# Stick-breaking's projections: the fourth pair's upper parts of q and k bound behind the rounding of the next column's weights

## The chip, the core and the metric

The kernel runs on one core of a Trainium2 chip. Its engines work side by side, each through its own list of instructions in order: TensorE (PE in the profile) multiplies matrices into PSUM, VectorE (DVE), ScalarE (ACT) and GpSimd (POOL) work elementwise, SyncE (SP) issues transfers; GpSimd's list holds transfers too. An instruction starts when its engine has come to it and the semaphores that it waits for have reached their values. The metric is the device time in microseconds, as the median of several runs.

## The reference

One layer of a hybrid decoder, 1024 real tokens and 16 meta tokens of width 1024, all in float32:

```python
h = h + 0.5 * swiglu(rms_norm(h, ffn1_norm), ffn1_w_in, ffn1_w_out)
u = rms_norm(h, mix_norm) @ w_in
hq, hf, hi, hg, sq, sk, sv = split(u)            # seven groups of 512 columns
o_hg = hgrn2(hq, hf, hi, hg, ...)                # 4 heads of 128, gated recurrence
o_sb = stick_breaking(sq, sk, sv, q_gain, k_gain)  # 8 heads of 64
h = h + concat(o_hg, o_sb) @ w_out
h = h + 0.5 * swiglu(rms_norm(h, ffn2_norm), ffn2_w_in, ffn2_w_out)
```

Stick-breaking normalizes q and k by head (`q = rms_norm(q, q_gain)`), forms scores `z = q k / 8`, and weights each earlier key with sigmoid(z) times the product of sigmoid(−z) over the keys between.

## The kernel before

Every float32 product is made of three products of rounded parts: an operand is split into an upper part (rounded, written by ScalarE) and a lower part (the rest, written by VectorE). For weights this is `split_w` (L231 rounds, L233 takes the rest); the tiles are `raw` (as loaded by SP, L226, two buffers), `wh` and `wl`. `self.rounded` always holds the last rounding of weights that the program has written down.

The stage that matters here is the projection `u`, column block by column block of 128. First come stick-breaking's columns, in four pairs of heads: for each pair k, v and q (`sb_project`), each in chunks of tokens. Then come hgrn2's, head by head in the order v, f, q, g (`hgrn_fill`): a v or f column in four pieces of 264, 264, 256 and 256 tokens, a q or g column in two of 512. Two PSUM banks take turns (`proj`), so the third piece of a column needs the first piece's bank to be emptied: ScalarE copies v out (L1108), and applies sigmoids to f (L1114, L1115). The next column's weights are rounded one column ahead. The first hgrn2 column's copies are bound behind the rounding that `kept["round"]` names.

Beside the projections runs, for each pair, `sb_qk`: it transposes q and k into a layout by rows, squares and sums, takes the root on ScalarE (L1434), scales by the inverse on GpSimd (L1438), transposes back on VectorE (L1444) into the tiles `qT` and `kT`, and calls `put_split` four times (two halves of q, two of k). `put_split` writes the upper part on ScalarE (L1375, tile `ohi`, three buffers), the lower part on VectorE (L1376, `olo`), and stores both from GpSimd's list (L1379, L1380) to DRAM, from where the heads load them later. `sb_v` does the same for v through `vhl` (L1396) and stores from SP (L1404).

When two hgrn2 columns (v and f of head 0) are written down, the memory of these stages is closed and the attention proper begins (`braid`): jobs of two query blocks each, whose scores `z` (L1598), the two sigmoids (`keep` L1604, `sig` L1605), scan on VectorE (L1608) and product on GpSimd (L1614) are woven into the remaining hgrn2 columns. Its tiles take over the memory just left, with waits for whoever used it last; GpSimd first sets the last column of `keep` to one (L1593). `sig` is then turned by TensorE (`flip`, L1453) and copied out of PSUM (`wu`, L1576 and L1577).

What sets the order: on TensorE the order of the code. On the other engines a scheduler sets it when the program is built, bound by data and by edges that the code gives: `with tc.issue_after(ins)` puts the instructions of its block that run on `ins`'s engine behind `ins` in that engine's list. It is no semaphore; it moves places in a list.

Of the kernel before, what the change touches and what calls it, by code (L numbers as in the profile page):

```python
# [40 lines left out]
class Block:  # L41
# [1368 lines left out]
    def sb_qk(self, p, qT, kT, pool, mix, dst):  # L1410

        nc = self.nc
        ss, other = (
            pool.tile([P, 65], F32, tag=x, name=x, bufs=2) for x in ("sbs", "sbo")
        )
        nat = pool.tile([P, 65, 32], F32, tag="nat", name="nat", bufs=2)  # L1420
        rows = [(qT, 0, 0, 16), (qT, 512, 16, 16), (kT, 0, 32, 16), (kT, 512, 48, 17)]
        for src, c0, b0, nb in rows:
            y = nat[:, b0 : b0 + nb]
            nc.vector.transpose(y.rearrange("p b d -> p (b d)"), src[:, c0 : c0 + 32 * nb])
            sq = pool.tile([P, 17, 32], F32, tag="sq4", name="sq4", bufs=2)[:, :nb]
            nc.scalar.activation(sq, y, AF.Square)
            nc.vector.tensor_reduce(ss[:, b0 : b0 + nb], sq, mybir.AxisListType.X, ALU.add)
            yield 0, 1500
        for b in range(4):
            nc.scalar.copy(  # L1430
                other[32 * b : 32 * b + 32], ss[32 * (b ^ 1) : 32 * (b ^ 1) + 32]
            )
        nc.vector.tensor_add(ss, ss, other)
        nc.scalar.activation(ss, ss, AF.Sqrt, bias=self.eps, scale=1.0 / 64)  # L1434
        nc.vector.reciprocal(ss, ss)
        for _, _, b0, nb in rows:
            y = nat[:, b0 : b0 + nb]
            nc.gpsimd.tensor_mul(  # L1438
                y, y, ss[:, b0 : b0 + nb].unsqueeze(2).broadcast_to([P, nb, 32])
            )  # L1440
        yield 0, 6000
        for src, c0, b0, nb in rows:
            t = src[:, c0 : c0 + 32 * nb]
            nc.vector.transpose(t, nat[:, b0 : b0 + nb].rearrange("p b d -> p (b d)"))  # L1444
            n = min(32 * nb, (SEQ if src is qT else T) - c0)
            gain, to = (self.qg8, dst[0]) if src is qT else (self.kg, dst[1])
            self.put_split(to, p, slice(c0, c0 + n), t[:, :n], mix, gain)
            yield 0, 1500

    def flip(self, src, spans):  # L1450
# [887 lines left out]
```

## Time and profile before

| what | value |
|---|---|
| median of 3 runs | 1991.07 us (1990.67 to 1992.21) |
| the profiled execution's own time | 1989.35 us |
| its span, first to last instruction | 1987.6 us |
| granted TensorE clock, mean over the span | 0.997 |
| TensorE busy | 1937.9 us, 97% |
| VectorE, ScalarE, GpSimd busy | 1390.7, 854.6, 448.0 us |

A row in the order of time gives start and duration in microseconds, the engine, the line, the operation, the tiles written and read, and in brackets how long the engine stood idle before and what released it. "SPq" and "POOL DMA" rows are the issue of a transfer; the time to landing is given in the view of transfers. The projections of the fourth pair and of the first hgrn2 columns lie between about 820 and 875 us, the attention follows.

### The profile page before, as it was taken

The numbers are of one execution on the slowest core, as the hardware profiler recorded it, in microseconds if no ns is written. First come the engines' busy times: TensorE is split into PE (matmuls) and PEld (weight loads), VectorE is DVE, ScalarE is ACT, GpSimd is POOL, SyncE is SP. The second block draws the span as 40 slices with busy tenths as digits, with TensorE's granted clock in tenths as the row PEclk, the third lists the DMA queues.
The fourth block names the chain that finished last, engine by engine and source line by source line (L and its number), as shares of the span: only waits on it lengthen the run. The fifth ranks groups of instructions, "written<-read, shape, count | busy, mean of one in ns | idle before, by whom it ended". The sixth has DMA issues, their size and how long they took to land.

```text
span 1987.6 us, 30439 instructions
## 1 busy us (share of the span) xinstructions
PE 1937.9 (97%) x10768; PEld 1631.7 (82%) x10768; DVE 1390.7 (70%) x2176; ACT 854.6 (43%) x1719; POOL 448.0 (23%) x616
## 2 busy tenths in 40 slices
PE   7999999999999999989999999999999999999998
PEld 6888888888888888878898978787888888888887
DVE  7977777877677765457777667567566766767774
ACT  6523443334444444356666635433233332344443
POOL 3010100010000003133333332220544544520000
PEclk9999999999999999989999999999999999999999
DMA  7356887758965225665453176665533323278463
GB/s 210 91 168 167 254 273 241 242 183 318 374 206 187 88 73 151 153 175 146 131 152 114 58 261 188 149 228 180 185 96 106 106 96 112 101 265 302 123 195 138
DMA packets 346168, 347.16 MB, mean 175 GB/s; under 512 B 94800, under 2 KB 250320, under 8 KB 346016
## 3 DMA queue, kind: packets, MB, share of 16 engines
q1 hardware_dynamic: 325168, 283.73, 46.4%
q0 software_dynamic: 19808, 61.49, 9.0%
q8 instruction: 85, 1.39, 0.3%
q14 instruction: 67, 0.55, 0.1%
q10 hardware_dynamic: 1040, 0.00, 0.0%
HBM read 233.75 MB, written 111.38 MB: 174 GB/s over the span
## 4 chain that ended last, share of the span: by engine, by line
PE 89%; DVE 5%; ACT 2%; DMA 2%; issue 1%; POOL 1%; SPq 0%; DVEq 0%; ACTq 0%; POOLq 0%
PE o L723 21%; PE qb L448 17%; PE qa L448 12%; PE qc L448 12%; PE proj L248 5%; PE proj L250 4%; PE proj L249 4%; PE flip L1453 2%; PE wo L248 1%; PE wo L249 1%; PE wo L250 1%; PE oacc L1528 1%; PE mq L992 1%; PE oacc L1530 1%; PE lvl L1225 1%
## 5 line engine op out<-in xcount | busy, mean ns | idle before, releaser
L448 PE MATMUL qb<-T,wh 128*128 128x512 f32 x1056 | 344.4, 390 | 1.4 <-ACT T L308 0.8
L448 PEld LDWEIGHTS qb<-T,wh 128*128 128x128 f32 x1056 | 198.1, 188 | 46.1 <-issue 2.5
L448 PE MATMUL qa<-B,wh 128*128 128x512 f32 x696 | 226.7, 390 | 0.1
L248 PE MATMUL proj<-xh,wh 128*128 128x512 f32 (+2 forms) x640 | 214.2, 335 | 10.8 <-ACT st L1108 9.7
L723 PE MATMUL o<-t,w 128*128 128x512 f32 x924 | 211.8, 390 | 0.5 <-DVE u L541 0.5
L250 PE MATMUL proj<-xl,wh 128*128 128x512 f32 (+2 forms) x640 | 210.4, 329 | 0.8 <-DVE xl L1917 0.8
L249 PE MATMUL proj<-xh,wl 128*128 128x512 f32 (+2 forms) x640 | 210.4, 329 | 0.0
L723 PE MATMUL o<-parts 128*128 128x512 f32 x924 | 209.9, 389 | 0.0
L448 PE MATMUL qb<-T,wl 128*128 128x512 f32 x528 | 205.4, 389 | 0.0
L723 PEld LDWEIGHTS o<-t,w 128*128 128x128 f32 x924 | 172.8, 188 | 37.3 <-issue 0.8
L723 PEld LDWEIGHTS o<-parts 128*128 128x128 f32 x924 | 173.3, 188 | 36.0
L361 DVE TENSOR_TENSOR wl<-s,wh 128x512 fp32r<-128x512 f32 x160 | 165.7, 1035 | 50.6 <-ACT wh L359 49.7
L359 ACT CAST wh<-s 128x512 fp32r<-128x512 f32 x160 | 99.4, 622 | 193.5 <-PE qb L448 145.1
L448 PEld LDWEIGHTS qa<-B,wh 128*128 128x128 f32 x696 | 130.5, 188 | 27.6 <-DVE B L827 0.5
L248 PEld LDWEIGHTS proj<-xh,wh 128*128 128x128 f32 x640 | 121.3, 190 | 22.9 <-ACT st L1108 9.9
L359 ACT CAST wh<-raw 128x512 fp32r<-128x512 f32 x120 | 74.4, 621 | 148.3 <-PE qc L448 108.0
L448 PE MATMUL qa<-B,wl 128*128 128x512 f32 x348 | 135.5, 389 | 0.0
L250 PEld LDWEIGHTS proj<-xl,wh 128*128 128x128 f32 x640 | 121.1, 189 | 12.2 <-DVE xl L1917 1.2
L249 PEld LDWEIGHTS proj<-xh,wl 128*128 128x128 f32 x640 | 121.2, 189 | 9.9
L448 PE MATMUL qc<-T,wh 128*128 128x512 f32 x352 | 117.1, 394 | 0.0
L1614 POOL TENSOR_TENSOR sig<-sig,keep 128x144 f32<-128x144 f32 (+3 forms) x64 | 82.1, 1283 | 154.5 <-DVE keep L1608 103.8
L448 PE MATMUL qc<-B,wh 128*128 128x512 f32 x352 | 115.0, 390 | 1.6 <-DVE u L541 1.6
(398 smaller groups left out, 3882.8 us busy)
## 6 DMA issues: line engine op xcount, KB each, us to landing
raw<-in_ffn_w_in_dram SPq DMA_DIRECT2D x176, 256.0 KB, 4.0
raw<-in_ffn_w_out_dram SPq DMA_DIRECT2D x112, 256.0 KB, 4.3
w2in<-both SPq DMA_DIRECT2D x28, 512.0 KB, 3.4
raw<-in_w_in_dram SPq DMA_DIRECT2D x25, 512.0 KB, 5.0
ks<-kD SPq DMA_DIRECT2D x32, 260.0 KB, 4.8
wout<-both SPq DMA_DIRECT2D x16, 512.0 KB, 3.9
wh<-w2in SPq DMA_DIRECT2D x27, 256.0 KB, 3.2
wl<-w2in SPq DMA_DIRECT2D x27, 256.0 KB, 3.4
```

The costliest lines, as they stand in the source:

```text
L248: nc.tensor.matmul(ps, wh[:, s], xs, start=k == 0, stop=False)
L249: nc.tensor.matmul(ps, wl[:, s], xs, start=False, stop=False)
L250: nc.tensor.matmul(ps, wh[:, s], xl[:, k, c0 : c0 + n], start=False, stop=k == nk - 1)
L359: nc.scalar.copy(hi, src)
L361: nc.vector.tensor_sub(lo, src, hi.bitcast(F32))
L448: nc.tensor.matmul(ps, a[:, k, :], b[:, k, :], start=start and k == 0 and i == 0, stop=k == 3 and i == 2, skip_group_check=True,)
L723: nc.tensor.matmul(banks[bank][m], y[:, m * P : (m + 1) * P], z, start=start and at == 0 and e == 0, stop=q == nq - 1 and e == 2, skip_gro ...
L992: nc.tensor.matmul(ps[at : at + 32, at_g, :], self.xm[:, 4 * h + k, :], got[i, h][:, k, :], start=h == 0 and kk == 0, stop=h == 1 and kk = ...
L1225: nc.tensor.matmul(ps[:, :, c, :], kp[:, P * c : P * c + P], strided(QA, P * c + n, (512 - n, 2), (2 * n, nb), (1, n)), start=True, stop=True,
L1453: self.nc.tensor.transpose(ps[:m, j, :], src[:, s0 : s0 + m], self.ident)
L1528: nc.tensor.matmul(o[:, c], vj, w[0], start=j == 0, stop=False, skip_group_check=True)
L1614: nc.gpsimd.tensor_mul(sig, sig, keep[:, 1 : nk + 1])
```

## The change

In `sb_qk`, for the fourth pair alone (`p == 3`), the call of `put_split` is put under an edge behind `self.rounded`, the last rounding of weights written down by then. Only instructions on that rounding's engine, ScalarE, get the edge: the four upper parts. VectorE's lower parts and GpSimd's stores follow through data. The transposes (L1444) are outside the block.

```diff
             n = min(32 * nb, (SEQ if src is qT else T) - c0)
             gain, to = (self.qg8, dst[0]) if src is qT else (self.kg, dst[1])
-            self.put_split(to, p, slice(c0, c0 + n), t[:, :n], mix, gain)
+            with self.tc.issue_after(self.rounded.ins) if p == 3 else ExitStack():
+                self.put_split(to, p, slice(c0, c0 + n), t[:, :n], mix, gain)
             yield 0, 1500
```

ScalarE's list before, from the root of the fourth pair on. `qT_7947` and `kT_7945` are the fourth pair's tiles; `wh_8255` are the rounded weights of hgrn2's first f column, `proj_8259` to `proj_8373` the four pieces of its first v column:

```order
L1434 ACTIVATE sbs_8246<-sbs_8246,eps_70 128x65
L1375 ACTIVATE ohi_8498<-qT_7947,qg8_82 128x512
L1375 ACTIVATE ohi_8538<-qT_7947,qg8_82 128x512
L1375 ACTIVATE ohi_8565<-kT_7945,kg_81 128x512
L1396 CAST vhl_8366<-vt_8345 128x32
L1375 ACTIVATE ohi_8572<-kT_7945,kg_81 128x528
L231 CAST wh_8255<-raw_8253 128x1024
L1108 COPY st_8284<-proj_8259 128x264
```

The same place after the change (lines below L1447 have a number higher by one):

```order
L1434 ACTIVATE sbs_8246<-sbs_8246,eps_70 128x65
L1396 CAST vhl_8366<-vt_8345 128x32
L231 CAST wh_8255<-raw_8253 128x1024
L1108 COPY st_8284<-proj_8259 128x264
L1108 COPY st_8325<-proj_8293 128x264
```

The four upper parts are gone from there. Further on in ScalarE's list, at the end of the f column and the start of the attention, before (`wh_8414` belongs to head 0's q column, `wh_8598` to its g column):

```order
L231 CAST wh_8414<-raw_8412 128x1024
L1114 ACTIVATE st_8516<-proj_8484 128x256
L1115 ACTIVATE st_8517<-proj_8484 128x256
L1114 ACTIVATE st_8556<-proj_8524 128x256
L1115 ACTIVATE st_8557<-proj_8524 128x256
L1604 ACTIVATE keep_8585<-z_8588 128x144
L1605 ACTIVATE sig_8586<-z_8588 128x144
L231 CAST wh_8598<-raw_8596 128x1024
L1604 ACTIVATE keep_8615<-z_8618 128x272
```

And after:

```order
L231 CAST wh_8414<-raw_8412 128x1024
L1375 ACTIVATE ohi_8498<-qT_7947,qg8_82 128x512
L1114 ACTIVATE st_8516<-proj_8484 128x256
L1115 ACTIVATE st_8517<-proj_8484 128x256
L1375 ACTIVATE ohi_8538<-qT_7947,qg8_82 128x512
L1114 ACTIVATE st_8556<-proj_8524 128x256
L1115 ACTIVATE st_8557<-proj_8524 128x256
L1375 ACTIVATE ohi_8565<-kT_7945,kg_81 128x512
L231 CAST wh_8598<-raw_8596 128x1024
L1375 ACTIVATE ohi_8572<-kT_7945,kg_81 128x528
L1605 ACTIVATE keep_8585<-z_8588 128x144
L1606 ACTIVATE sig_8586<-z_8588 128x144
```

The four upper parts stand behind `wh_8414`, the rounding that the edge names, and the attention's first two sigmoids have moved behind `wh_8598` and the last upper part. VectorE's list at the same place, before:

```order
L2140 MEMSET idle_8583 128x1
L1608 SCALAR_TENSOR_TENSOR keep_8585<-keep_8585,idle_8583 128x144
L233 TENSOR_TENSOR wl_8600<-raw_8596,wh_8598 128x1024
L1608 SCALAR_TENSOR_TENSOR keep_8615<-keep_8615,idle_8583 128x272
L1608 SCALAR_TENSOR_TENSOR keep_8626<-keep_8626,idle_8583 128x457
```

and after:

```order
L2141 MEMSET idle_8583 128x1
L233 TENSOR_TENSOR wl_8600<-raw_8596,wh_8598 128x1024
L1376 SCALAR_TENSOR_TENSOR olo_8573<-kT_7945,kg_81,ohi_8572 128x528
L1609 SCALAR_TENSOR_TENSOR keep_8585<-keep_8585,idle_8583 128x144
L1609 SCALAR_TENSOR_TENSOR keep_8615<-keep_8615,idle_8583 128x272
```

The last lower part and the rest of the weights now stand ahead of the attention's first scan. The lists of TensorE and GpSimd hold the same rows in the same order; SP's differs in a few places of the attention (stores of f ahead of stores of k, loads of v ahead of a store of q).

## The prediction

> **What bounds the kernel now.** I read the page first, then TensorE's waits, then the two stretches that the change touches in order of time, engine by engine.
>
> ```profile
> span 1987.6 us, 30439 instructions
> PE 1937.9 (97%) x10768; PEld 1631.7 (82%) x10768; DVE 1390.7 (70%) x2176; ACT 854.6 (43%) x1719; POOL 448.0 (23%) x616
> ```
>
> TensorE is busy for 97% of the span, so the kernel gets faster only where TensorE stands still or runs slowly. In the stretch from 700 to 860 us its waits hold one large entry:
>
> ```profile
> PE proj L248 <- ACT st L1108: 9.7, 1, 9.7
> ```
>
> That is one wait of 9.7 us, for a copy of a product out of PSUM on ScalarE. The order of time shows it, on TensorE and then on ScalarE (start, duration, in brackets the idle time before; the last matmul had ended at 852.50 − 9.73 = 842.77):
>
> ```profile
> 852.50 0.58 PE L248 MATMUL proj<-xh,wh 128*128 128x256 f32 x1 [9.73 <-ACT st L1108]
> ```
>
> ```profile
> 842.53 0.35 ACT L1434 ACTIVATE sbs<-sbs,eps 128x65 f32<-128x65 f32 x1 [0.36 <-DVE sbs L1433]
> 845.45 0.72 ACT L1375 ACTIVATE ohi<-qT,qg 128x512 fp32r<-128x512 f32 x1 [2.57 <-DVE qT L1444]
> ...
> 848.08 0.20 ACT L1396 CAST vhl<-vt 128x32 fp32r<-128x32 f32 x1
> 850.50 0.73 ACT L1375 ACTIVATE ohi<-kT,kg 128x528 fp32r<-128x528 f32 x1 [2.22 <-DMA qD<-ohi]
> 851.14 1.03 ACT L231 CAST wh<-raw 128x1024 fp32r<-128x1024 f32 x1
> 852.08 0.65 ACT L1108 COPY st<-proj 128x264 f32<-128x264 f32 x2
> 857.08 0.37 ACT L1108 COPY st<-proj 128x256 f32<-128x256 f32 x1 [4.36 <-PE proj L250]
> 859.92 0.37 ACT L1108 COPY st<-proj 128x256 f32<-128x256 f32 x1 [2.46 <-PE proj L250]
> ```
>
> Both projection banks are full at 842.77. The copy that empties the first (852.08) stands on ScalarE behind a rounding of weights (851.14), and that behind the fourth pair's four upper parts (L1375, 845.45 to 850.50), which wait for transposes (2.57 us) and for a store to land (2.22 us). So it is the place of the four in ScalarE's queue, not their work, that holds TensorE.
>
> The stop costs more than its length. The columns of the view by stretches: the stretch, its length, TensorE's busy time and instructions, granted clock, DMA share, GB/s.
>
> ```profile
> 842.80:845.20 2.40, 0.00 (x0) 1.00 0.00 0
> 845.20:845.60 0.40, 0.00 (x0) 0.90 0.00 0
> 852.50:857.10 4.60, 4.60 (x26) 0.65 1.04 286
> ...
> 1290.20:1291.80 1.60, 0.00 (x0) 1.00 0.47 83
> ```
>
> Some 2.4 to 2.8 us into the idle time the granted clock falls, and the third piece of the column (24 matmuls) then takes 857.08 − 852.50 = 4.58 us, where the fourth, just like it, takes 859.92 − 857.08 = 2.84 us. That is 1.74 us lost to the low clock. A stop of 1.6 us (at 1290) left the clock at 1.00.
>
> **The change, part by part.** No instruction is added or removed. The four upper parts (ScalarE), the four lower parts behind them (VectorE) and their eight stores (GpSimd's queue) move; the order on TensorE and GpSimd stays. The rows of the lists are those shown with the change.
>
> Three sets of rows for (1): the last issues on SP ahead of the stop, then, over the whole program, how long the 48 stores of v's parts (L1404) and the 25 loads of these weights (L226) took to land.
>
> ```profile
> 828.37 2.23 SPq L1404 DMA_DIRECT2D vD<-vhl  x4
> 830.65 0.63 SPq L226 DMA_DIRECT2D raw<-in_w_in_dram  x1
> ```
>
> ```profile
> DMA to landing us min/median/max: 1.4/3.0/6.9
> ```
>
> ```profile
> DMA to landing us min/median/max: 3.6/5.0/8.9
> ```
>
> (1) *The wait at 842.77 shrinks.* ScalarE is free at 842.53 + 0.35 = 842.88. `vhl` costs 0.20 less some 0.05 of overlap, the rounding to the copy 852.08 − 851.14 = 0.94, the copy to TensorE 852.50 − 852.08 = 0.42: TensorE restarts at about 844.4, 8.1 us earlier, after 1.6 us of idle time. Are the inputs there? `vhl` at 848.08 had no idle time before it, so the trace does not say since when it was ready. The two things it could wait for are old: the four stores that free its buffer were issued from 828.37 to 830.6 and the weights at 830.65, and the longest landing times of those stores and loads (6.9 and 8.9 us) end by 839.6.
>
> (2) *The clock stays up*, since 1.6 us is what 1290 survived: 1.7 us more. Together −9.9 us.
>
> (3) *A new wait, at the start of the attention.* Before, `keep_8585` and `sig_8586` came ahead of `wh_8598`. Now they come behind it and the last upper part, and `sig_8586` also waits for the last lower part, `olo_8573`: the attention's tiles take over the memory of `kT`, which that step reads. The first three upper parts of 0.72 each lie between the f column's pieces, where ScalarE waits for TensorE (1.99 before 871.45), and cost nothing; the fourth is behind a load:
>
> ```profile
> 868.21 5.05 DMA raw<-in_w_in_dram
> ...
> 871.45 0.39 ACT L1114 ACTIVATE st<-proj 128x256 f32<-128x256 f32 x1 [1.99 <-PE proj L250]
> 872.16 0.31 ACT L1605 ACTIVATE sig<-z 128x144 f32<-128x144 f32 x1
> 873.28 1.05 ACT L231 CAST wh<-raw 128x1024 fp32r<-128x1024 f32 x1 [0.81 <-DMA raw<-in_w_in_dram]
> ...
> 852.23 0.77 DVE L1376 SCALAR_TENSOR_TENSOR olo<-kT,kg,ohi 128x528 fp32r<-128x528 f32 x1 [1.89 <-ACT wh L231]
> 874.37 1.23 DVE L233 TENSOR_TENSOR wl<-raw,wh 128x1024 fp32r<-128x1024 f32 x1 [1.17 <-ACT wh L231]
> 875.51 5.83 DVE L1608 TENSOR_TENSOR_SCAN keep<-keep,idle 128x272 f32<-128x272 f32 x6
> ...
> 874.62 0.46 PE L1598 MATMUL z<-ks,qs 128*128 128x456 f32 x1
> 875.59 0.47 PE L1598 MATMUL z<-ks,qs 128*128 128x456 f32 x1 [0.24 <-ACT sig L1605]
> ```
>
> In the old times: the load lands at 873.26, the rounding follows, its low part holds VectorE until 875.51, `olo_8573` takes 0.77 to 876.28, `sig_8586` 0.31 to 876.6. TensorE's third score (874.62) needs the PSUM bank that `sig_8586` reads, so it starts at 876.65: 2.0 us late. From there ScalarE sets the pace of the scores (TensorE waits at 875.59 already), so nothing is won back.
>
> The load may land later than 5.05 us, because the stores of the first upper and lower parts now run beside it (before, only projection stores and a load of q did). The third pair shows such a load, issued among that pair's own stores, and its landing time (last number):
>
> ```profile
> 816.74 0.55 SPq L226 DMA_DIRECT2D raw<-in_w_in_dram  x1
> ...
> 817.21 0.54 POOL L1379 DMA_DIRECT2D kD<-ohi  x1 [0.65 <-ACT kT L1337]
> ```
>
> ```profile
> raw<-in_w_in_dram SPq DMA_DIRECT2D x1, 512.0 KB, 6.3
> ```
>
> I take 6.3, the nearest row: 1.25 us more. The new wait is 2.0 + 1.25 = 3.3 us, between 2.0 and, at the longest landing of 8.9 us, 5.9.
>
> (4) *GpSimd's queue.* Behind the eight stores stand the attention's three memsets of `keep` and its products:
>
> ```profile
> 853.29 0.54 POOL L1380 DMA_DIRECT2D kD<-olo  x1 [1.22 <-DVE olo L1376]
> 853.82 0.19 POOL L1593 MEMSET keep<- 128x1 f32 x3
> 873.35 0.43 POOL L1614 TENSOR_TENSOR sig<-sig,keep 128x144 f32<-128x144 f32 x1 [19.34 <-DVE keep L1608]
> ```
>
> The cover was 19 us; now the last store goes out at 876.28 and the memsets end at 877.0, so VectorE's scans start 0.7 us after `olo_8573` and run 1.9 us behind 875.51, no later than TensorE's own lateness under (3). I cost it at nothing beside (3). The q and k of the fourth pair are read only by the last two of eight heads, so the stores' lateness itself costs nothing.
>
> (5) *A second rounding moves.* In the attention, ScalarE's list now reads
>
> ```order
> L231 CAST wh_8882<-raw_8880 128x1024
> L1577 CAST wu_8745<-flip_8787 128x4x128
> ```
>
> where before the copy stood nine rows ahead of the rounding. On SP, three loads of v now stand ahead of the q store of 883.95, and the weights `raw_8880` right behind it. The old times of the store, the load (with its landing time) and the copy, and TensorE's waits for such copies in the attention:
>
> ```profile
> 883.95 0.33 SPq L1124 DMA_DIRECT2D hg_q<-st  x1
> ...
> 886.32 1.17 SPq L226 DMA_DIRECT2D raw<-in_w_in_dram  x2
> ```
>
> ```profile
> 889.32 0.61 ACT L1576 CAST wu<-flip 128x512 fp32r<-128x512 f32 x1
> ```
>
> ```profile
> raw<-in_w_in_dram SPq DMA_DIRECT2D x1, 512.0 KB, 5.7
> ```
>
> ```profile
> PE flip L1453 <- DVE wu L1577: 2.9, 7, 0.7
> ```
>
> Issued at 884.35 the weights land at 890.0 (5.7 us) and are rounded by 891.0: the copy is 1.7 us late. TensorE has other work in between, so 0 to 1.7; I take 0.7, the longest wait that it ever had for such a copy.
>
> *Sum:* −8.1 − 1.7 + 3.3 + 0.7 = −5.8, with the rounding of the terms −5.9 us. The profiled execution took 1989.35 us (span 1987.6 and 1.75 around it) and would take 1983.45; it lies 1.72 us under the median of the three runs, 1991.07, from which the same sum gives **1985.2 us**. A change of 0.2% (4.0 us) is about what a measurement of this kernel can tell.
>
> **The rivals.**
> *The new wait is hidden* (the load is on time, `olo_8573` fits a gap): −9.9 + 0.7 = −9.2, 1981.9 us. Against it: in the old times the load alone lands 1.3 us before TensorE needs the bank, and 3.0 us of rounding, low part and `olo_8573` follow.
>
> *The clock falls again* in the new wait. A wait of 3.3 us is longer than the 2.4 to 2.8 us after which it fell at 842.8; the scores behind it are paced by ScalarE, so the loss is between 0 and the 1.74 us seen there, say 1.4: 1986.6 us. The Trainium skill (TensorE: Matmul & The Clock Gate, "HAM oscillation — how this bites in real kernels") sets the limit at idle gaps of about 3.4 us, with a free-running window; by that page the 3.3 us would just pass at full clock. The trace's fall came earlier than the page's limit, so I give the fall a chance.
>
> *Late weights.* If `raw_8596` lands after 8.9 us, the wait is 5.9: −9.9 + 5.9 + 0.7 = −3.3, 1987.8 us, no difference that can be told.
>
> *Slower.* The same mechanism decides this side: every microsecond of lateness of `raw_8596` now stops ScalarE, VectorE and the scores. From −7.2 at 5.05 us, the kernel is 4.0 us slower once the load takes 5.05 + 11.2 = 16.3 us, for example 1996 us at 17 us. None of 25 loads took over 8.9.
>
> *The change doesn't do what it says:* `vhl` or the rounding is held past 848 by something that the trace doesn't show, and TensorE waits as before: within 1991 ± 3 us. The issue times under (1) speak against it.
>
> **How the numbers follow.** The forecast 0.53 (its own range 1984.0 to 1986.3, landing between 5.05 and 7.4 us without a fall of the clock), hidden 0.13, clock 0.17, late weights 0.09, no effect 0.03, slower 0.05. Faster by over 0.2% is the first three, 0.83; within 0.2% late weights and no effect, 0.12; slower 0.05. The range 1981.8 to 1987.4 takes in the first three and leaves out 0.17.
>
> **What would show it.** In the profile after: TensorE's wait for L1108 near 1.6 us with the clock at 1.00 behind it and 2.8 us for the third piece; upper parts of the fourth pair between the f column's sigmoids; a new TensorE wait of 2.0 to 3.3 us for a `sig` before the third score; the load `raw` before it landing in 5 to 6.5 us; a short ScalarE wait for weights some 15 us later. The prediction is wrong if the first wait is still several microseconds, or the new one is over 6 us, or the clock falls there.

## The result and the profile after

The changed kernel takes 1989.41 us (median of 22 runs, 1987.14 to 1991.66), the kernel before, beside it, 1992.02 us. The ratio is 0.9987 with a 95% interval of 0.9981 to 0.9993: 2.6 us faster (1.4 to 3.8), less than the 0.2% that the forecast took as telling. A second series gave 0.9992 (0.9983 to 1.0001). Forecast were −5.9 us and a range that ended at 1987.4.

The two profiled executions are no help at their ends: their spans are 1987.6 us before and 1987.7 us after. Further on, the changed one waits 1.1 us for a load of `w_out` (`PE wo L248 <- DMA wh<-wout`); the kernel before has that wait in its second profile (1.0 us) and not in its first, so it belongs to the execution and not to the change. So the places are compared, by the same instruction in both. First TensorE's waits after, from 835 to 900 us (engine, line and tile that waited, what it waited for: us in total, times, longest):

```profile
PE z L1599 <- ACT sig L1606: 6.5, 4, 5.6
PE proj L248 <- ACT st L1108: 1.5, 1, 1.5
PE flip L1454 <- DVE wu L1578: 1.3, 1, 1.3
```

The wait of 9.7 us has become one of 1.5 us, as forecast. In its place stands a wait of 5.6 us for a `sig`, where 3.3 was forecast. ScalarE in the order of time, at both places:

```profile
843.27 0.35 ACT L1434 ACTIVATE sbs<-sbs,eps 128x65 f32<-128x65 f32 x1 [0.35 <-DVE sbs L1433]
843.52 0.20 ACT L1396 CAST vhl<-vt 128x32 fp32r<-128x32 f32 x1
843.63 1.04 ACT L231 CAST wh<-raw 128x1024 fp32r<-128x1024 f32 x1
844.58 0.65 ACT L1108 COPY st<-proj 128x264 f32<-128x264 f32 x2
848.11 0.37 ACT L1108 COPY st<-proj 128x256 f32<-128x256 f32 x1 [2.88 <-PE proj L250]
...
865.53 1.05 ACT L231 CAST wh<-raw 128x1024 fp32r<-128x1024 f32 x1 [1.79 <-DMA raw<-in_w_in_dram]
866.49 0.73 ACT L1375 ACTIVATE ohi<-kT,kg 128x528 fp32r<-128x528 f32 x1
867.12 0.27 ACT L1605 ACTIVATE keep<-z 128x144 f32<-128x144 f32 x1
871.07 0.29 ACT L1606 ACTIVATE sig<-z 128x144 f32<-128x144 f32 x1 [3.68 <-DVE olo L1376]
```

The first five rows are the forecast's steps: `vhl`, rounding and copy follow the root without a gap, and the third piece is done at 848.11. In the last four the load of weights is nearly where it was forecast (landed at 865.5), but behind `keep` ScalarE stands for 3.68 us until the last lower part, `olo`, is written. VectorE shows why that is late:

```profile
866.61 1.23 DVE L233 TENSOR_TENSOR wl<-raw,wh 128x1024 fp32r<-128x1024 f32 x1 [2.02 <-ACT wh L231]
870.21 0.77 DVE L1376 SCALAR_TENSOR_TENSOR olo<-kT,kg,ohi 128x528 fp32r<-128x528 f32 x1 [2.37 <-DMA qD<-olo]
```

`wl` is done at 867.84, and then VectorE waits 2.37 us for a store, `qD<-olo`. The tile `olo` has three buffers and the fourth pair has four lower parts: the fourth takes the first one's buffer, and may do so only when the first has been stored. The chain of the stretch (start, length, what):

```profile
862.31 7.81 DMA qD<-olo
...
870.21 0.78 DVE olo L1376
...
871.07 0.30 ACT sig L1606
...
871.42 0.75 PE z L1599
```

The store was issued at 862.31 and took 7.81 us to land. In the kernel before the same store took 3.35 us; its row in the view of transfers (KB each, us to landing):

```profile
qD<-olo POOLq DMA_DIRECT2D x1, 256.0 KB, 3.3
```

Last, the granted clock of TensorE around the new wait (stretch, length, busy time and instructions, clock, DMA share, GB/s):

```profile
865.80:870.40 4.60, 0.04 (x1) 1.00 1.05 340
870.40:870.60 0.20, 0.00 (x0) 0.79 0.98 319
870.60:877.20 6.60, 5.37 (x15) 0.50 1.02 323
877.20:877.40 0.20, 0.20 (x3) 0.65 0.74 218
```

The clock was at half for 6.8 us. From the third score to the first projection behind the scores TensorE needs 877.60 − 871.42 = 6.18 us, before 879.53 − 874.62 = 4.91 us: the low clock costs 1.27 us. (Where the clock stayed up behind the same wait, in the first execution with four `olo` buffers below, it is 871.33 − 866.44 = 4.89 us.)

```profile
877.60 0.48 PE L248 MATMUL proj<-xh,wh 128*128 128x512 f32 x1
```

```profile
879.53 0.48 PE L248 MATMUL proj<-xh,wh 128*128 128x512 f32 x1
```

### The profile page after: what moved, and what is told of

Read it like the earlier page. It is cut to its first block, busy times and chain, and to the rows that moved or that the text cites. A ratio compares the mean times of both kernels' runs of the same rounds, so it can differ in the third digit from the quotient of the medians.

```text
span 1987.7 us, 30439 instructions
## 1 busy us (share of the span) xinstructions
PE 1938.9 (98%) x10768; PEld 1631.7 (82%) x10768; DVE 1390.3 (70%) x2176; ACT 854.7 (43%) x1719; POOL 449.4 (23%) x616
## 4 chain that ended last, share of the span: by engine, by line
PE 89%; DVE 4%; DMA 3%; ACT 2%; issue 1%; POOL 1%; SPq 0%; DVEq 0%; ACTq 0%; POOLq 0%
PE o L723 21%; PE qb L448 18%; PE qa L448 12%; PE qc L448 12%; PE proj L248 4%; PE proj L250 4%; PE proj L249 4%; PE flip L1454 2%; PE wo L248 1%; PE wo L249 1%; PE wo L250 1%; PE mq L992 1%; PE oacc L1529 1%; PE oacc L1531 1%; PE z L1599 1%
## 5 line engine op out<-in xcount | busy, mean ns | idle before, releaser
L248 PE MATMUL proj<-xh,wh 128*128 128x512 f32 (+2 forms) x640 | 213.5, 334 | 2.6 <-ACT st L1108 1.5
L248 PEld LDWEIGHTS proj<-xh,wh 128*128 128x128 f32 x640 | 120.6, 188 | 14.7 <-ACT st L1108 1.7
L448 PEld LDWEIGHTS qb<-T,wl 128*128 128x128 f32 x528 | 99.1, 188 | 20.2
```

What stands on the lines that cost most here:

```text
L248: nc.tensor.matmul(ps, wh[:, s], xs, start=k == 0, stop=False)
L448: nc.tensor.matmul(ps, a[:, k, :], b[:, k, :], start=start and k == 0 and i == 0, stop=k == 3 and i == 2, skip_group_check=True,)
```

## The experiments

Three theories. **A:** the new wait is the last lower part's wait for its buffer, that is for the first lower part's store, which is late because other transfers run beside it; the fall of the clock comes on top. **B:** the late weights and their rounding ahead of the sigmoid make the wait. **C:** the stretch does win what it should, and the program gives it back later.

| kernel | median us (runs) | ratio to before (95%) | wait before the third score, us |
|---|---|---|---|
| before | 1992.0 / 1991.0 / 1990.9 | 1 | none |
| changed | 1989.41 (22) | 0.9987 (0.9981 to 0.9993) | 5.58 |
| changed, again | 1989.15 (11) | 0.9992 (0.9983 to 1.0001) | 4.82 |
| one `vt` buffer | 1989.72 (11) | 0.9989 (0.9981 to 0.9998) | 4.07 |
| one `vt`, four `olo` buffers | 1985.54 (5) | 0.9966 (0.9953 to 0.9978) | 1.23, 2.06, 2.60 |
| later loads | 1986.93 (11) | 0.9981 (0.9973 to 0.9990) | 2.48 |
| q early | 1981.39 (5) | 0.9949 (0.9936 to 0.9963) | none |
| all behind the second copy | 1982.41 (5) | 0.9952 (0.9940 to 0.9964) | none |
| spread over the copies | 1981.21 (5) | 0.9945 (0.9931 to 0.9958) | none |

The three times of the kernel before are those beside the changed kernel and in the two series of experiments. "None" means no more than the 0.2 to 0.5 us between scores that the kernel before has too.

**A fourth buffer.** Memory had no room for it, so v's tile `vt` gave up one of its two; the control gives up the same buffer and nothing else.

```diff
-        lo = pool.tile([P, n], F32R, tag="olo", name="olo", bufs=bufs)
+        lo = pool.tile([P, n], F32R, tag="olo", name="olo", bufs=bufs + (gain is not None))
...
-            y = mix.tile([P, nb, 32], F32, tag="vt", name="vt", bufs=2)
+            y = mix.tile([P, nb, 32], F32, tag="vt", name="vt", bufs=1)
```

> The changed kernel, with a fourth buffer for the lower parts of q and k (olo); to make room, v's tile vt has one buffer instead of two. Theory A (the new wait is the last lower part waiting for its buffer, that is for the store of the first lower part, which lands 7.8 us after its issue): that wait is gone, the load of weights, which landed at 865.5, is what is left: rounding to 866.6, the rest of the weights to 867.8, the lower part 0.77, the sigmoid 0.31, so TensorE's wait before the third score falls from 5.6 us to about 3, the granted clock stays near 1.00 behind it, and the time is 2.5 to 4 us below the changed kernel's (about 1986 us). Rival B (the late weights and their rounding make the wait): it stays at 5 to 6 us, and the time at about 1989. Rival C (the time that the stretch wins is given back later in the program): the wait shrinks as under A, and the time still stays within 1 us of the changed kernel's.

> The changed kernel with one buffer for v's tile vt and nothing else: the control for the fourth olo buffer. All theories: within 1 us of the changed kernel (about 1989.4 us), the wait before the third score 5 to 6 us. If it is slower by more than 1 us, that is the price of the lost buffer, and the kernel with four olo buffers is to be compared with this one.

The control takes the time of the changed kernel, 1989.72 us. Its wait, 4.07 us, is shorter than the 5 to 6 expected, since in that execution the store landed in 5.96 us; the store still ends it. The fourth buffer takes 4.2 us off the control. VectorE's row for the last lower part has no wait for a store any more, although the first lower part's store landed at 867.52, after that part had begun:

```profile
865.24 0.76 DVE L1376 SCALAR_TENSOR_TENSOR olo<-kT,kg,ohi 128x528 fp32r<-128x528 f32 x1
866.10 0.29 ACT L1606 ACTIVATE sig<-z 128x144 f32<-128x144 f32 x1 [1.15 <-DVE olo L1376]
866.44 0.47 PE L1599 MATMUL z<-ks,qs 128*128 128x456 f32 x1 [1.23 <-ACT sig L1606]
```

But this execution took 1982.3 us and was the fastest of five that reached up to 1987.3. What the usual ones look like, two more profiles were to show.

> The kernel with four olo buffers once more: its profiled execution took 1982.3 us, its five runs 1982.3 to 1987.3. Theory A: where the execution is slower, the load of weights ahead of the last upper part lands later than the 862.99 of the first profile (up to 865.5 as in the changed kernel), the wait before the third score is then 2 to 3.5 us, and the clock may fall behind it; the store of the first lower part does not end it. Rival B' (the store matters even with a fourth buffer): a wait ended by the landing of a store.

> The same kernel for a third profile: as for the second, a wait of 1.2 us with a time near 1982 when the weights land by 863, a wait of 2 to 3.5 us with a time of 1985 to 1987 when they land later or the clock falls.

Both took 1985.3 us. The weights landed at 863.87 and 863.42 (862.99 in the first profile), the waits were 2.06 and 2.60 us, no store ended them, and the clock fell behind both, for 6.8 us each. In each of the three the third score starts 3.44 or 3.45 us after the landing of the weights (866.44, 867.32 and 866.86), so here it is that landing which sets the wait. What was expected of this kernel, a wait of about 3 us and the clock up, was too long for the wait and right for the clock in one profile of three. From the second profile, ScalarE's and TensorE's rows:

```profile
863.89 1.05 ACT L231 CAST wh<-raw 128x1024 fp32r<-128x1024 f32 x1 [0.74 <-DMA raw<-in_w_in_dram]
866.97 0.29 ACT L1606 ACTIVATE sig<-z 128x144 f32<-128x144 f32 x1 [1.22 <-DVE olo L1376]
867.32 0.48 PE L1599 MATMUL z<-ks,qs 128*128 128x456 f32 x1 [2.06 <-ACT sig L1606]
```

So with the store out of the way the path that the forecast had costed is what remains (weights, rounding, rest, last lower part, sigmoid), at 1.2 to 2.6 us, and the clock goes in two profiles of three. B is not the cause of the 5.6 us, but it is what lies under it.

**Fewer transfers beside the store.** The loads of the second head's q and k wait on SP until behind the last store of the f column:

```diff
-            nc.sync.dma_start(dst[kind][h, :, s], t)
+            self.stored = nc.sync.dma_start(dst[kind][h, :, s], t)
...
-                    ahead = load(*heads[i + 1])
+                    with self.tc.issue_after(self.stored.ins) if i == 0 else ExitStack():
+                        ahead = load(*heads[i + 1])
```

> The changed kernel, with the loads of the second head's q and k held on SP until behind the last store of the f column, so that fewer transfers run beside the store of the first lower part. Theory A with crowding (that store needs 7.8 us instead of the 3.4 us of the kernel before because the loads share the DMA engines): it lands 1 to 4 us sooner, TensorE's wait before the third score falls to 3 to 4.5 us, and the time by 1 to 3 us against the changed kernel. Theory A without crowding (the store is late because of its own queue): the landing stays over 7 us, the wait at 5 us or more, the time within 1 us of the changed kernel's 1989.4. In both the loads come later, which could cost time in the attention; a wait on ks or qs would show that.

The store landed 4.9 us after its issue, the wait was 2.48 us (shorter than the 3 to 4.5 expected), and the time fell by 2.2 us against the changed kernel of the same series (1986.93 to 1989.15). The transfer rows of the store in the changed kernel and here:

```profile
qD<-olo POOLq DMA_DIRECT2D x1, 256.0 KB, 7.8
```

```profile
qD<-olo POOLq DMA_DIRECT2D x1, 256.0 KB, 4.9
```

The view by stretches, each from the issue of the store to its landing, before, changed and here:

```profile
848.79:852.14 3.35, 0.00 (x0) 0.50 0.96 338
```

```profile
862.31:870.12 7.81, 3.53 (x20) 2.81 (x18) 2.71 (x5) 3.13 (x6) 2.74 (x6) 1.00 1.03 308
```

```profile
860.64:865.56 4.92, 3.75 (x21) 3.02 (x20) 2.71 (x5) 3.13 (x6) 2.61 (x6) 1.00 1.07 372
```

The busy times of the engines stand in the middle (in the first row TensorE's alone), the last two numbers of a row are the DMA share and GB/s. The engines of the DMA are full in all three (shares of 0.96, 1.03 and 1.07); what differs is how much passes until the 256 KB are down: 3.35 us × 338 GB/s = 1.1 MB before, 2.4 MB in the changed kernel, 1.8 MB here. The store is late because it shares full engines with more transfers, among them the next heads' q and k. The landing alone sets the wait, as four executions show:

| execution | store issued | took | landed | third score | between |
|---|---|---|---|---|---|
| changed | 862.31 | 7.81 | 870.12 | 871.42 | 1.30 |
| changed, again | 861.98 | 7.57 | 869.55 | 870.85 | 1.30 |
| one `vt` buffer | 862.12 | 5.96 | 868.08 | 869.38 | 1.30 |
| later loads | 860.64 | 4.92 | 865.56 | 866.86 | 1.30 |

**q early.** The two upper parts of q go behind the second copy of the first v column, the two of k stay behind the rounding. No buffer is added. The lines taken out, here and in the next two edits, are those of the changed kernel; `self.copied` is a list that starts empty:

```diff
-                nc.scalar.copy(t, ps)
+                self.copied.append(nc.scalar.copy(t, ps))
...
-            with self.tc.issue_after(self.rounded.ins) if p == 3 else ExitStack():
+            with self.tc.issue_after((self.copied[1] if b0 < 32 else self.rounded).ins) if p == 3 else ExitStack():
```

> The two upper parts of q bound behind the second copy of the first v column, the two of k behind the rounding as in the changed kernel. The first lower part is stored some 11 us sooner, so the last lower part's buffer is free without a fourth one; the load of weights, its rounding and the last lower part still stand ahead of the first sigmoid. Theory A: the wait before the third score falls from 5.6 us to between 1 and 3.3 us (the load's landing decides), the clock stays up, 2.5 to 5 us under the changed kernel (1984.5 to 1987 us). Rival B (the load, the rounding and the last upper part in front of the sigmoid make the wait): 5 us or more, the time near 1989.

It went better than A had it: the first lower part was issued at 850.15 and landed in 3.7 us, and in this order ScalarE and VectorE come to the last upper and lower part before the rounding, in gaps where they waited anyway, so the weights are out of the path too. Its waits from 835 to 900 us:

```profile
PE proj L248 <- ACT st L1108: 1.5, 1, 1.5
PE z L1600 <- ACT sig L1607: 1.0, 3, 0.5
PE flip L1455 <- DVE wu L1579: 0.4, 1, 0.4
```

The first wait is as in the changed kernel, the second is gone, and 8.0 us of time with it (1989.4 to 1981.4).

**All four ahead of the attention.** Two kernels put the four upper parts behind copies of the v column: all behind the second copy, or spread (two behind the second, one behind the third, one behind the fourth). Both keep the list `self.copied`.

```diff
-            with self.tc.issue_after(self.rounded.ins) if p == 3 else ExitStack():
+            with self.tc.issue_after(self.copied[1].ins) if p == 3 else ExitStack():
```

```diff
-            with self.tc.issue_after(self.rounded.ins) if p == 3 else ExitStack():
+            with self.tc.issue_after(self.copied[max(1, b0 // 16)].ins) if p == 3 else ExitStack():
```

> The kernel before, with the four upper parts bound behind the second copy of the first v column (L1108) instead of behind the rounding. Removes the first wait as the change does, and keeps the upper parts ahead of the attention. Theory A: first wait about 1.6 us, no wait before the third score beyond the 0.2 to 0.5 us of the kernel before; the last upper part, behind a store, holds the third copy for about 1.5 us: 8 us under the kernel before (about 1984 us). Rival B says the same of this kernel, since the rounding of the g column's weights is back behind the first sigmoids. Rival C: the stretch wins 8 us up to the third score, but no more than 3 us are left at the end (1989 us or above).

> As the one with all four behind the second copy, but spread: the first two upper parts behind the second copy of the v column, the third behind the third copy, the fourth behind the fourth. Theory A: no stop but the first of about 1.6 us and none before the third score, so 9 to 10 us under the kernel before (about 1982.5 us), the fastest of all. Rival B: the same. Rival C: no more than 3 us under the kernel before (1989 us or above).

They take 1982.41 and 1981.21 us. With all four behind the second copy, the last one waits for a store and holds the third copy, so TensorE has a second stop (2.9 us in two waits); spread, it has none longer than 0.3 us. TensorE's waits from 835 to 900 us, first of the one, then of the other:

```profile
PE proj L248 <- ACT st L1108: 2.9, 2, 1.5
PE z L1600 <- ACT sig L1607: 1.2, 4, 0.5
PE flip L1455 <- DVE wu L1579: 0.4, 1, 0.4
```

```profile
PE proj L248 <- ACT st L1108: 1.5, 1, 1.5
PE z L1600 <- ACT sig L1607: 1.2, 4, 0.5
PE flip L1455 <- DVE wu L1579: 0.4, 1, 0.4
PE proj L248 <- ACT st L1115: 0.3, 1, 0.3
```

C falls: what the stretch wins stays won. The spread kernel is 9.8 us faster than the one before (1990.99 in its series; ratio 0.9945, 0.9931 to 0.9958), and q early is as good; both beat the kernel before and the changed one.

**The same two again.**

> The changed kernel once more, as it is, for a second profile of the same chip session: how far the new wait, the landing time of the first lower part's store and the fall of the clock vary from one execution to the next. Theory A: a wait of 4 to 6.5 us, always ended by the landing of that store and the lower part behind it, and a fall of the clock each time; the time within 1 us of 1989.4.

> The kernel before once more, for a second profile: the wait of 9.7 us, the fall of the clock behind it and the third score without a wait should come again within a few tenths of a microsecond, since none of them hangs on a transfer; the whole time may vary by 2 us.

The changed kernel's second profile shows a wait of 4.82 us ended by the same store (7.57 us), and the clock at half for 6.8 us. The kernel before repeats its wait of 9.7 us and has no wait before the third score; its span was 1987.7 us. Its stop costs the same each time, the changed kernel's hangs on a landing.

## Why the prediction was wrong

(1) *The first wait* was right: 1.49 us against 1.6. As it was 9.73, the step gave 8.24 us, forecast 8.1. The spread kernel tests steps (1) and (2) without the rest: −9.8 us measured, −8.1 − 1.7 forecast.

(2) *The clock stays up* was right, the term of 1.74 us a little too large: the third piece ran from 845.00 to 848.11, 3.11 us against 4.58 before, so 1.47 and not 1.74. The 2.84 us of the fourth piece that the forecast compared it with ran from copy to copy, the 4.58 from TensorE's first matmul to the copy, which also holds one matmul's own 0.28 us.

(3) *The new wait* is the step that failed. It was costed at 3.3 us, as the weights, their rounding, their rest, `olo_8573` and `sig_8586` in a row. That row exists, and alone it is worth 1.2 to 2.6 us. But `olo_8573` waits for a second thing, its buffer, and that ended last: 5.58, 4.82 and 4.07 us in three profiles. The sentence that was wrong stands in step (4): "The q and k of the fourth pair are read only by the last two of eight heads, so the stores' lateness itself costs nothing." The data are read late, but the buffer is wanted at once. The forecast's own rows had shown the ring closing late, on both engines. On ScalarE the last upper part stood 2.22 us for `DMA qD<-ohi`. On VectorE the last lower part stood 1.89 us before 852.23; the view puts that down to `wh`, which `olo` doesn't read. The upper part that it reads was done at 851.23, and the first lower part's store landed at 848.79 + 3.35 = 852.14, 0.09 us before `olo` began, just as in the changed kernel (870.12 and 870.21). In the third pair of the kernel before, the view names the store:

```profile
818.37 0.77 DVE L1376 SCALAR_TENSOR_TENSOR olo<-kT,kg,ohi 128x528 fp32r<-128x528 f32 x1 [0.44 <-DMA qD<-olo]
```

So the change did not make the wait for the buffer. Before, nothing that TensorE needed stood behind it. Moved, it stands ahead of a sigmoid that TensorE waits for, and beside the attention's loads, where the store takes 7.81 us instead of 3.35. The spread kernel shows the first half of this by itself: VectorE waits 3.0 us there for the same store, and TensorE loses nothing by it.

(4) For the rest GpSimd's queue behaved nearly as worked out: the scans started 0.98 us after the last lower part, where 0.7 was put, and none of TensorE's waits up to 893 is for a scan.

(5) *The second rounding* was put at 0.7 us, as weights that come late and delay a copy on ScalarE. The weights did not come late: the rounding starts without idle time.

```profile
887.39 1.06 ACT L231 CAST wh<-raw 128x1024 fp32r<-128x1024 f32 x1
888.34 0.60 ACT L1577 CAST wu<-flip 128x512 fp32r<-128x512 f32 x1
```

The copy `wu` behind it is late by the rounding's 0.95 us, but it is not what TensorE waits for. With the rounding the rest of those weights, `wl`, has moved forward on VectorE, and there it holds what follows:

```profile
888.49 2.34 DVE L233 TENSOR_TENSOR wl<-raw,wh 128x1024 fp32r<-128x1024 f32 x1 [0.25 <-ACT wh L231]
890.75 0.68 DVE L1578 TENSOR_TENSOR wu<-flip,wu 128x512 fp32r<-128x512 f32 x1
...
892.23 0.66 DVE L1123 TENSOR_TENSOR st<-st,proj 128x512 f32<-128x512 f32 x1
892.81 0.68 DVE L1578 TENSOR_TENSOR wu<-flip,wu 128x512 fp32r<-128x512 f32 x1
```

VectorE comes to its own `wu` at 890.75, although the copy was done at 888.94. The product of L1123 starts 1.72 us after ScalarE's L1122 (890.51); in the kernel before, where `wl` came later, it started 0.64 us after it (892.43 to 893.07). TensorE waits for the last of these rows: 1.29 us where it was 0.38, so 0.91. That this is near the 0.7 is luck, since the way to it was another. In all the profiles in which that rounding stands ahead of that copy (changed twice, one `vt`, four `olo` three times, later loads) the wait is 1.3 us, in those in which it stands behind (before, q early, both copies kernels) 0.4.

*The rival "the clock falls again"* came true beside the failed step, and cost 1.27 us where 1.4 was put. It was given 0.17; it fell in each of six profiles with a stop of 2.06 us or more at this place, and not in the one of 1.23. Its limit was too high: the forecast took the 2.4 to 2.8 us after which the clock fell at 842.8, and stops of 2.06 us and of 2.48 lost it as well. "Late weights" is nearest to the measured change (−3.3 us against −2.6), but by luck: the weights landed where the forecast had them, and the wait was for a buffer.

The sum with what was measured in this pair: −8.24 − 1.47 + 5.58 + 1.27 + 0.91 = −1.95 us, forecast −5.9. The turned tiles behind the wait start at 893.63 where they started at 894.50, and this execution had come to the first stop 0.74 us later than the other (843.51, 842.77): −1.6 us, so the terms hold to 0.35 us. The medians' −2.6 (−1.4 to −3.8) takes in both.

## What to carry to other kernels

An instruction that is moved behind something takes its buffer ring with it: ask for every tile in the moved block how many buffers it has, which transfer must land before the first comes round again, and what else will be on the DMA engines at that time. Late data that nobody reads yet are free; a late buffer is free only while nothing that the busiest engine needs stands behind the instruction that wants it. And where a block is moved off one stop, spread it over the gaps just behind that stop before moving it to the next crowded place: the same four instructions gave 2.6 us there and 9.8 us spread.

## What was not expected of the hardware

The time at half clock comes in steps. The limits are read from slices of 0.2 us, in which the mean clock tells when it changed:

| execution | stop, us | clock fell | rose | low for |
|---|---|---|---|---|
| before | 842.77 to 852.50 | 845.52 | 855.76 | 10.24 |
| changed | 865.84 to 871.42 | 870.52 | 877.34 | 6.82 |
| changed, again | 866.03 to 870.85 | 870.93 | 877.76 | 6.83 |
| one `vt` buffer | 865.31 to 869.38 | 868.19 | 878.43 | 10.24 |
| later loads | 864.38 to 866.86 | 867.22 | 874.04 | 6.82 |
| later loads, further on | 1257.44 to 1259.48 | 1259.75 | 1263.16 | 3.41 |

The low times are one, two and three times 3.41 us, and in the one kernel with two falls these are 392.53 us apart, 115 times 3.413. The Trainium skill (TensorE: Matmul & The Clock Gate, "Part 1: The HAM clock gate") gives a free-running window of 3413 ns, and that much the traces bear out. A whole idle window was not needed, however: the fall at 1259.75 came at the end of 3.41 us of which 2.04 were spent in this stop, and after TensorE had started again. The stop and the fall, by stretches:

```profile
1257.44:1259.48 2.04, 0.00 (x0) 1.00 0.86 225
1259.60:1259.80 0.20, 0.20 (x1) 0.88 0.70 123
1259.80:1263.00 3.20, 3.20 (x9) 0.50 0.96 200
```

Stops of 1.49 us (the first wait, in every profile after) left the clock up; stops of 2.04, 2.06, 2.48 and 2.60 us did not. What counts is the idle time in one window. The stop of 1.64 us at 1290.20 in the kernel before lies within one, 1289.25 to 1292.67 when the windows are counted on from the fall at 845.52, and left the clock up. One of 1.78 us in the changed kernel's second profile (1261.89 to 1263.67) left it up too, but counted from that execution's fall at 870.93 a window ends at 1263.46, so only 1.57 us of it lie in one. That places the limit here between 1.6 and 2.0 us of idle time in one window. A stop of over 4.1 us then has 2.04 us or more in some window wherever it stands, and is sure to lose the clock; how late it falls (2.3 to 4.9 us into the stop) is a matter of where the window stands. The price varies with it: from the third score to the score of 264 columns behind the projection the kernel before needs 7.79 us, the executions with two low windows 1.27 to 1.92 us more, and the one-`vt` kernel with three 2.69 us more (10.48).
